# Key products of cross-attention's memory around the mixer's output projection, and decode rows broadcast by TensorE, in a one-layer decoder step

## The chip, the cores and the metric

The kernel runs on one core of one Trainium2 chip, in one launch. The metric is the device time of that launch in microseconds (us). The program has five instruction streams: PE (TensorE, matrix products; its weight loads are shown apart as PEld), DVE (VectorE, elementwise work and reductions), ACT (ScalarE, copies, casts, activations), POOL (GpSimd) and SP (SyncE, which here only issues DMA transfers). Each works through its own instructions in program order and waits on semaphores where it needs what another has made. Matrix products land in PSUM, which has eight banks of 128 partitions by 512 float32; all else is in SBUF or in DRAM.

## The reference

One step of a one-layer hybrid decoder trunk in float32, for a prompt of 512 tokens and 8 decode rows (one token each), 2048 features. Prompt and decode rows pass the weights together, as 520 columns.

```python
y, new = mixer(rmsnorm(x, w['g_mix']), ...)          # w_in, RG-LRU and mLSTM groups, w_out
x = x + y
x = x + cross_attn(rmsnorm(x, w['g_xattn']), mk, mv, w)
hf = rmsnorm(x, w['g_ffn'])
x = x + jnp.square(jax.nn.relu(hf @ w['w_up'])) @ w['w_down']

def mem_kv(mem, w):                                  # prompt only: 256 memory tokens
    mn = rmsnorm(mem, w['g_mem'])
    return (mn @ w['w_mk']).reshape(B, 256, 4, 512), (mn @ w['w_mv']).reshape(B, 256, 4, 512)

def cross_attn(h, mk, mv, w):                        # 4 heads of 512
    q = (h @ w['w_cq']).reshape(B, T, 4, 512)
    s = einsum('bthd,bnhd->bhtn', q, mk) * 512 ** -0.5
    p = softmax(s, axis=-1)
    return einsum('bhtn,bnhd->bthd', p, mv).reshape(B, T, 2048) @ w['w_co']
```

The prompt attends to keys and values made in this step from `mem_prompt` (`w_mk`, `w_mv`, also returned). The 8 decode rows attend to given caches `K` and `V` of 256 tokens each, one cache for each row.

## The kernel before, in words

**Precision.** Each float32 operand is split into a high part (rounded to fp32r) and a low part (the rest); a product is three matmuls: high by high, high by low, low by high. The high part is made by a copy on ACT, the low part by a subtraction on DVE. A weight tile is 128 x 1024 (512 KB); `split_weights` makes its pair (ACT L97, DVE L98).

**Stages.** `run_jobs` does `w_in` (82 jobs of 48 matmuls, L162) with the RG-LRU and mLSTM work between them as generators in `tasks`; one call of `step_tasks` before each job takes each a step further. Its SBUF tiles come from `slots`, 36 buffers of one tag; `hh` (the mLSTM output, two a head), `og`, `ta` and `tb` are among them. `pair_out` spills each finished pair of feature blocks to DRAM (`td["out"]`, L709 to L713). Then `rest` runs a list of jobs, `seq`: `w_out`, `w_cq`, keys and values of the memory, `w_co`, `w_up`, and four groups of `w_down`.

The big projections use Strassen's scheme with seven products for each two-by-two block (`strassen`): a unit is seven jobs, a job is 24 matmuls of 128 x 260 (`product`, L900). Each product needs its operand set (`set_load`): two batches of four feature-block pairs, each read from DRAM (520 KB, L824), copied (ACT L825) and subtracted (DVE L818) into tiles of the pool `ops` (28 buffers, `op_tile`). All seven sets of a stage, 28 tiles, stay for the whole stage. `w_out` has eight units, so have `w_cq` and `w_co`. In a stage's last unit, `leave` loads the next stage's set into the tiles that a product has just used; `set_tail` fills in the last unit's own part. The results accumulate in three PSUM tags, `acca`, `accb`, `accc`, two banks each; `ax` has two more. A unit's first product is evacuated (into `x` by DVE L907, or by ACT L918) before its third may add to the same bank.

**Order of transfers.** Every load and store is issued by SP, in one order. Weight tiles (`raw`, L844, seven buffers) are fetched one unit ahead, two jobs ahead they are split (`LOOK`). The order of all instructions on each engine is fixed when the program is built, by priorities: what stands in `high_priority` goes forward.

**Keys and values.** For each head in turn: eight jobs for the keys (`mk_job`, L1087: 24 matmuls of 256 columns, four blocks of 128 features, result `mkx[h]` kept in SBUF and stored to the output), then eight for the values (`mv_job`, L1110: 12 matmuls of 512 columns). The memory's own operands `mact` (8 tiles) are loaded in `w_cq`'s last unit (`mem_load`).

**Attention.** When a head's keys are done, `attn_prompt(h)` starts as a task: it loads the queries back (L1129), makes scores (L181), softmax, transposed probabilities, and, when the head's values and the decode are done, the weighted values; `mixed` and `spill` write `w_co`'s operands. For the decode rows, `attn_decode` takes one row of one cache at each step: `fetch` loads a cache tile (512 KB, `kv`, three buffers, L1026) and the row's query or probabilities, read from DRAM once for every partition (`qb`, two buffers, L1025); DVE multiplies and sums (L1035 for K, two of 512; L1054 for V, four of 256). `DRATE` is its steps for a job of cost 1: a product has cost 0.2, a key or value job 1.0. It begins when `w_cq`'s second unit is done. After the last value job `att_left` runs what is left of the tasks and then loads all of `w_co`'s sets.

## Time and profile before

| | us |
|---|---|
| median of 3 runs | 2968.2 (2967.15 to 2971.34) |
| the profiled execution | 2964.66 |
| its span, first to last instruction | 2962.9 |
| PE busy | 2700.3 (91% of the span) |
| PEld busy | 2626.2 (89%) |
| DVE busy | 2294.6 (77%) |
| ACT busy | 1344.3 (45%) |
| DMA, q1: 528.51 MB | 54.0% of 16 engines |

The profile shows one execution. Busy times of an engine are sums over its instructions; PE's are partly modelled, since matmuls overlap, and a matmul that starts late or at a lower granted clock counts as longer. A row of a group reads: line, engine, operation, tile written and tiles read, shape, count; then busy time, mean ns of one, and the idle time of the engine just before them with what ended it. A row of waits reads: who waited for whom, us in all, times, the longest. A row of windows has, for one stretch, the busy time of each engine with its instruction count, PE's granted clock, the share of the 16 DMA engines, and GB/s. In a timeline or a chain each row begins with start and length in us.

### The profile page before, as it was taken

To read this page: it belongs to the slowest core of one execution; us is meant where nothing else is said; L and a number is where in the kernel's file an instruction comes from. 1 tells how busy PE (TensorE), PEld (TensorE's weight loads), DVE (VectorE), ACT (ScalarE), POOL (GpSimd) and SP (SyncE) were. 2 spreads that over 40 slices of the span, in tenths; PEclk is the share of its full clock that TensorE was granted. 3 is DMA by queue.
4 is the path that set the end of the run, shared out by engine and by line. 5 is a ranking of instruction groups with operands and counts; after the bars stand their busy time and mean duration, and the time that the engine had idled before them with its cause. 6 is when DMAs were issued, how large, how long until landed. Compare 5 with 4: busy or idle time off the path is not lost.

```text
span 2962.9 us, 51442 instructions
## 1 busy us (share of the span) xinstructions
PE 2700.3 (91%) x20990; PEld 2626.2 (89%) x20990; DVE 2294.6 (77%) x3458; ACT 1344.3 (45%) x1759; POOL 31.3 (1%) x32
## 2 busy tenths in 40 slices
PE   7999999969979976796998999999998999989996
PEld 7999999968979955585997999999998989989896
DVE  7777887748878766666789777777778888887886
ACT  3444556425454421244445554554554343443543
POOL 2000000000000000000000000000000000000001
PEclk8999999989989988897998999999999999999998
DMA  4566542456666688884566655455457353443532
GB/s 142 184 212 206 187 152 87 152 200 200 197 215 213 196 260 262 276 279 164 189 208 241 203 165 164 147 162 165 148 166 261 100 201 100 151 143 107 187 108 79
DMA packets 224645, 531.80 MB, mean 179 GB/s; under 512 B 23692, under 2 KB 97132, under 8 KB 224408
## 3 DMA queue, kind: packets, MB, share of 16 engines
q1 hardware_dynamic: 224408, 528.51, 54.0%
q8 instruction: 165, 2.70, 0.4%
q14 instruction: 72, 0.59, 0.1%
HBM read 421.83 MB, written 106.73 MB: 178 GB/s over the span
## 4 chain that ended last, share of the span: by engine, by line
PE 66%; DVE 13%; DMA 12%; issue 4%; ACT 4%; SPq 1%; DVEq 0%; ACTq 0%; POOL 0%; POOLq 0%
PE acca L900 30%; PE accc L900 15%; PE mm L162 9%; PE accb L900 8%; DVE wlo L98 3%; DVE op L818 2%; DMA qb<-dp 1%; ACT whi L97 1%; DMA op<-tdd 1%; PE mv L1110 1%; DMA raw<-in_w_mv 1%; PE ax L181 1%; DVE raws L798 1%; DMA kv<-in_V 1%; PE mk L1087 1%
## 5 line engine op out<-in xcount | busy, mean ns | idle before, releaser
L900 PE MATMUL acca<-op,whi 128*128 128x260 f32 x5632 | 1051.3, 286 | 82.5 <-ACT t L918 20.2
L900 PEld LDWEIGHTS acca<-op,whi 128*128 128x128 f32 x5632 | 881.8, 190 | 92.0 <-DVE op L818 24.2
L900 PE MATMUL acca<-op,wlo 128*128 128x260 f32 x2816 | 804.1, 286 | 4.1 <-DVE wlo L98 3.9
L97 ACT CAST whi<-raw 128x1024 fp32r<-128x1024 f32 x416 | 436.4, 1050 | 607.0 <-PE acca L900 183.1
L98 DVE TENSOR_TENSOR wlo<-raw,whi 128x1024 fp32r<-128x1024 f32 x416 | 508.2, 1222 | 111.5 <-ACT whi L97 107.9
L900 PEld LDWEIGHTS acca<-op,wlo 128*128 128x128 f32 x2816 | 537.4, 191 | 5.0 <-DVE wlo L98 4.9
L900 PE MATMUL accc<-op,whi 128*128 128x260 f32 x2816 | 524.2, 284 | 11.3 <-DVE op L818 7.6
L97 ACT CAST whi<-raws 128x1024 fp32r<-128x1024 f32 x264 | 276.9, 1049 | 425.0 <-PE accc L900 137.7
L162 PE MATMUL mm<-xa,whi 128*128 128x260 f32 x2624 | 439.8, 289 | 21.3 <-ACT ssq L321 7.3
L900 PEld LDWEIGHTS accc<-op,whi 128*128 128x128 f32 x2816 | 439.5, 190 | 14.6 <-DVE op L818 9.8
L98 DVE TENSOR_TENSOR wlo<-raws,whi 128x1024 fp32r<-128x1024 f32 x264 | 322.9, 1223 | 134.2 <-ACT whi L97 133.8
L900 PE MATMUL accc<-op,wlo 128*128 128x260 f32 x1408 | 399.6, 284 | 0.7 <-DVE wlo L98 0.7
L162 PEld LDWEIGHTS mm<-xa,whi 128*128 128x128 f32 x2624 | 370.6, 192 | 26.1 <-DVE xa L310 7.4
L900 PE MATMUL accb<-op,whi 128*128 128x260 f32 x1408 | 272.3, 292 | 28.3 <-DVE op L818 16.7
L162 PE MATMUL mm<-xa,wlo 128*128 128x260 f32 x1312 | 270.8, 288 | 1.6 <-DVE wlo L98 1.6
L900 PEld LDWEIGHTS accc<-op,wlo 128*128 128x128 f32 x1408 | 266.8, 189 | 1.0 <-DVE wlo L98 0.9
L900 PEld LDWEIGHTS accb<-op,whi 128*128 128x128 f32 x1408 | 226.2, 195 | 32.5 <-DVE op L818 19.6
L162 PEld LDWEIGHTS mm<-xa,wlo 128*128 128x128 f32 x1312 | 206.3, 192 | 2.4 <-DVE wlo L98 2.1
L900 PE MATMUL accb<-op,wlo 128*128 128x260 f32 x704 | 203.4, 289 | 0.0
L818 DVE TENSOR_TENSOR op<-op,op 128x1040 fp32r<-128x1040 f32 (+2 forms) x132 | 156.6, 1190 | 26.6 <-ACT op L825 18.1
L97 ACT CAST whi<-wraw 128x1024 fp32r<-128x1024 f32 x82 | 85.5, 1045 | 151.0 <-PE mm L162 122.2
L825 ACT CAST op<-op 128x1040 fp32r<-128x1040 f32 x112 | 113.7, 1018 | 86.8 <-DMA op<-tdd 43.5
(328 smaller groups left out, 3097.7 us busy)
## 6 DMA issues: line engine op xcount, KB each, us to landing
raw<-in_w_up SPq DMA_DIRECT2D x128, 512.0 KB
raw<-in_w_down SPq DMA_DIRECT2D x128, 512.0 KB
wraw<-in_w_in SPq DMA_DIRECT2D x80, 512.0 KB
tdd<-w SPq DMA_DIRECT2D x32, 1040.0 KB
op<-tdd SPq DMA_DIRECT2D x56, 520.0 KB
raw<-in_w_out SPq DMA_DIRECT2D x32, 512.0 KB
raw<-in_w_cq SPq DMA_DIRECT2D x32, 512.0 KB
kv<-in_K SPq DMA_DIRECT2D x32, 512.0 KB
```

The costliest lines, as they stand in the source:

```text
L97: S.copy(hi, raw)
L98: V.tensor_tensor(out=lo, in0=raw, in1=hi.bitcast(F32), op=ALU.subtract)
L162: PE.matmul(ps[:, hf, 0:HT], w[:, j, :], x[:, HALF[hf]], start=(k == 0 and wi == 0), stop=(k == n - 1 and wi == 2))
L181: PE.matmul(out, u, v, start=first and i == 0, stop=last and i == 2)
L798: V.tensor_tensor(out=out, in0=x, in1=y, op=op)
L818: V.tensor_tensor(out=lo, in0=src, in1=hi.bitcast(F32), op=ALU.subtract)
L825: S.copy(hi[:, 0:n], lo[:, 0:n].bitcast(F32))
L900: PE.matmul(out, u[:, k], x[:, j], start=(new and k == 0 and i == 0), stop=(k == 7 and i == 2), skip_group_check=not new)
L1087: PE.matmul(st["mk"], u[:, i, :], x, start=(k == 0 and wi == 0), stop=(k == KB - 1 and wi == 2))
L1110: PE.matmul(st["mv"][i], x[:, ms], u[:, j], start=(k == 0 and wi == 0), stop=(k == KB - 1 and wi == 2))
```

## The change

Four things go together.

- The products for keys are taken out of the heads' order. Eight of the sixteen blocks (`MKEYS`) run before `w_out`, eight between `w_out` and `w_cq`. Each result goes through one buffer `sq` to the output and to DRAM (`dmk`). The memory's operands are loaded three times instead of once: before each key block and again in `w_cq`'s last unit. Of `w_out`'s and `w_cq`'s seven sets, five are loaded before or during a key block and two after it (`late_sets`), since the memory's tiles take eight of the 28 buffers.
- Decode rows are no longer read from DRAM for every partition. Queries and probabilities are split once a head (`rows_split`), and for each row TensorE writes it to all 128 partitions of an `acca` bank by two matmuls with one column of an identity, broadcast (`spread`); DVE reads it from PSUM. `qb` is gone, `kv` has four buffers, `t` two. `DRATE` is 1.5, and a value job has cost 1.5.
- Scores are a task of their own (`attn_scores`), two heads ahead of the weighted values at most (`attn_values`); both begin with the first value job. `w_co`'s first half of the sets is loaded before the last head's weighted values, the second after them, and two tails are filled from SBUF.
- In `w_in`, `slots` has 28 buffers; `hh` has a pool of eight of its own, `og`, `ta` and `tb` come from `kv`'s six.

```diff
-SLOTS = 36
+SLOTS = 28
...
-DRATE = 2.0
+DRATE = 1.5
+MKEYS = 8
...
+    phh = part1.enter_context(tc.tile_pool(name="phh", bufs=8))
...
-        hh = [slot("hh") for _ in range(2)]
+        hh = [phh.tile([P, T], F32, tag="hh", name=nm("hh")) for _ in range(2)]
...
-        ta, tb = slot("ta"), slot("tb")
+        ta, tb = stream((P, T)), stream((P, T))
...
-            t = slot("og")
+            t = stream((P, T))
...
+        def batch_load(key, s, b, n=4):
+            hi, lo = op_tile(), op_tile()
+            load(lo[:, 0:n].bitcast(F32), td[key][b][:, s, 0:n])
+            S.copy(hi[:, 0:n], lo[:, 0:n].bitcast(F32))
+            lo_of(lo[:, 0:n], lo[:, 0:n].bitcast(F32), hi[:, 0:n])
+            sets.setdefault((key, s), []).append((hi, lo))
...
+                if nxt == "cq":
+                    st["wcq"] = st_["w"]
+                    set_tail(nxt, 3, st_["w"], slots=SLOT_OF[:5])
+                else:
+                    set_tail(nxt, 3, st_["w"])
...
+            def leave(s):
+                p = SLOT_OF.index(s)
+                if nxt != "cq":
+                    set_load(nxt, s, 3)
+                elif p < 2:
+                    mem_load(2 * p)
+                    mem_load(2 * p + 1)
+                else:
+                    set_load(nxt, SLOT_OF[p - 2], 3)
+
...
-            enter("b", t=3, kv=3, qb=2, r=1, sm=1)()
+            enter("b", t=2, kv=4, r=1, sm=1)()
...
-            def fetch(b, rows, n, src):
-                q, t = tl("qb", (P, 512)), tl("kv", (P, 1024))
-                load(q[:, 0:n], rows_of(rows, b * n, n))
-                load(t, src[h, b].rearrange("p a b -> p (a b)"))
-                return q, t
-
-            cur = [fetch(b, dqd[h], 512, a["K"]) for b in range(2)]
+            sc = sm_tile("sc", (P, 2, NB))
+
+            def rows_split(n, src, dst):
+                hi, lo = (sm_tile("row" + c, (NB, 512), F32R)[:, 0:n] for c in "hl")
+                if dst is None:
+                    load(lo.bitcast(F32), src)
+                    src = lo.bitcast(F32)
+                S.copy(hi, src)
+                lo_of(lo, src, hi)
+                return hi, lo
+
+            def fetch(b, src):
+                t = tl("kv", (P, 4 * HT))[:, 0:1024]
+                load(t, flat(src[h, b]))
+                return t
+
+            def spread(rows, b, n):
+                ps = pacc.tile([P, 512], F32, tag="acca", name=nm("row"))[:, 0:n]
+                for i, r in enumerate(rows):
+                    PE.matmul(ps, identr[0:NB, b:b + 1].to_broadcast([NB, P]), r, start=i == 0, stop=i == 1)
+                return ps
+
+            q = rows_split(512, dqd[h], None)
+            cur = [fetch(b, a["K"]) for b in range(2)]
             for b in range(NB):
                 yield
-                qb, kt = cur.pop(0)
+                kt, qb = cur.pop(0), spread(q, b, 512)
                 for i in range(2):
                     t = kt[:, i * 512:(i + 1) * 512]
                     V.tensor_tensor_reduce(out=t, in0=t, in1=qb, op0=ALU.mult, op1=ALU.add,
                                            scale=1.0, scalar=0.0, accum_out=sc[:, i, b:b + 1])
                 if b + 2 < NB:
-                    cur.append(fetch(b + 2, dqd[h], 512, a["K"]))
-            for _ in range(4):
+                    cur.append(fetch(b + 2, a["K"]))
+            cur = [fetch(b, a["V"]) for b in range(2)]
+            for _ in range(2):
                 yield
             tp = ax()
             for i in range(2):
                 PE.transpose(out=tp[0:NB, i * P:(i + 1) * P], in_=sc[:, i], identity=ident)
-            pd = stage["sm"].tile([NB, NMEM], F32, tag="pd", name=nm("pd"))
+            pd = sm_tile("pd", (NB, NMEM))
             softmax(tp[0:NB, 0:NMEM], NB, pd)
-            dp = dram.tile([NB, NMEM], F32, name=nm("dp"))
-            load(dp, pd)
-            cur = [fetch(b, dp, NMEM, a["V"]) for b in range(2)]
+            p = rows_split(NMEM, pd, True)
+            yield
             for b in range(NB):
                 yield
-                pb, vt = cur.pop(0)
+                vt, pb = cur.pop(0), spread(p, b, NMEM)
                 for j in range(4):
                     t = vt[:, j * NMEM:(j + 1) * NMEM]
-                    V.tensor_tensor_reduce(out=t, in0=t, in1=pb[:, 0:NMEM], op0=ALU.mult, op1=ALU.add,
...
+        dmk = [dram.tile([P, 4, NMEM], F32, name=f"dmk{h}") for h in range(4)]
...
-        def mk_post(h, j, g):
+        def mk_post(n, g):
             if g:
-                if j == 0:
-                    mkx[h] = op_tile((P, 4, NMEM), F32)
-                t = mkx[h][:, j]
+                t = tl("sq", (P, NMEM))
                 V.tensor_tensor(out=t, in0=st["mk"], in1=rm, op=ALU.mult)
-                load(o["mk"][4 * h + j], t)
-                if j == 3:
-                    start(attn_prompt(h))
+                load(o["mk"][n], t)
+                load(dmk[n // 4][:, n % 4], t)
 
...
         def mv_post(h, g):
             if g == 7:
-                mvx[h] = op_tile((P, 2, 512), F32)
+                while h > 1 and not pv_done[h - 2]:
+                    step_tasks()
+                t = tl("kv", (P, 4 * HT))[:, 0:1024].rearrange("p (a b) -> p a b", a=2)
                 for i in range(2):
-                    t = mvx[h][:, i]
-                    S.activation(t, st["mv"][i], AF.Copy, scale=rmc[:, i:i + 1])
-                    load(o["mv"][h, i], t)
+                    S.activation(t[:, i], st["mv"][i], AF.Copy, scale=rmc[:, i:i + 1])
+                    load(o["mv"][h, i], t[:, i])
+                mvx[h] = hi, lo = op_tile((P, 2, 512)), op_tile((P, 2, 512))
...
+        def attn_scores():
+            for h in range(4):
+                while h > 1 and not pv_done[h - 2]:
+                    yield
...
+                pTs[h] = pT
+
+        def attn_values():
+            for h in range(4):
+                while not (adec_done[h] and h in mvx and h in pTs):
+                    yield
...
+                        wa, wb = (op_tile(dt=F32) if h < 3 else tl("kv", (P, 4, HT)) for _ in range(2))
...
+                pv_done[h] = True
+
+        def att_enter():
+            start(attn_scores())
+            start(attn_values())
 
         def att_left():
+            while not (pv_done[2] and 3 in pTs):
+                step_tasks()
+            for s in SLOT_OF:
+                batch_load("co", s, 0)
             while tasks:
                 step_tasks()
-            for _, _, s in ORDER:
-                set_load("co", s, 3)
-            set_tail("co", 3, *wlast)
+            for s in SLOT_OF:
+                batch_load("co", s, 1, 2)
+            for j in range(2):
+                set_tail("co", 2 + j, *wlast[j])
...
+        def keys(n0, n1):
+            plain([a["w_mk"][n, g] for n in range(n0, n1) for g in range(2)],
+                  lambda g, w: mk_job(n0 + g // 2, g % 2, w), lambda g: mk_post(n0 + g // 2, g % 2))
+
+        def late_sets(key, last):
+            def go():
+                for s in SLOT_OF[5:]:
+                    set_load(key, s, last)
+                if last < 4:
+                    set_tail(key, 3, st["wcq"], slots=SLOT_OF[5:])
+            return go
+
+        def mem_again(s):
+            p = SLOT_OF.index(s)
+            if p < 2:
+                mem_load(2 * p)
+                mem_load(2 * p + 1)
+
+        keys(0, MKEYS)
+        seq[-1]["after"] = late_sets("out", 4)
+        strassen("out", 8, sq_src("w_out"), **residual(0, 1, C_X, "cq"))
+        keys(MKEYS, KB)
+        seq[-1]["after"] = late_sets("cq", 3)
+        strassen("cq", 8, sq_src("w_cq"), ev_q, cq_enter, mem_again)
+        first = len(seq)
         for h in range(4):
-            plain([a["w_mk"][4 * h + j, g] for j in range(4) for g in range(2)],
-                  lambda g, w, h=h: mk_job(h, g // 2, g % 2, w), lambda g, h=h: mk_post(h, g // 2, g % 2))
             plain([a["w_mv"][h, g] for g in range(8)],
                   lambda g, w, h=h: mv_job(h, g, w), lambda g, h=h: mv_post(h, g))
+        seq[first]["enter"] = att_enter
...
+        enter("a", x=2, w=2, sq=1, ss=1)()
         for q in range(4):
             fetch(0, q)
-        for _, _, s in ORDER:
-            set_load("out", s)
+        for k4 in range(4):
+            mem_load(k4)
         for n in range(LOOK):
             prep(n)
+        for s in SLOT_OF[:5]:
+            set_load("out", s)
```

More of the change, by code (lines that the diff above doesn't have):

```diff
@@ L72, in stream @@
     def stream(shape):
-        return small.tile(list(shape), F32, tag="kv", name=nm("kv"), bufs=6)
+        return small.tile([P, T], F32, tag="kv", name=nm("kv"), bufs=6)[:, 0:shape[1]]
     def aux():
@@ L270, in tile_trunk @@
     rm = keep.tile([P, NMEM], F32, name="rm")
+    identr = keep.tile([NB, NB], F32R, name="identr")
     drows = dram.tile([4, 3, TP], F32, name="drows")
@@ L818, in lo_of, with set_tail @@
             V.tensor_tensor(out=lo, in0=src, in1=hi.bitcast(F32), op=ALU.subtract)
-        def set_load(key, s, last=4):
-            out = []
-            for b, n in ((0, 4), (1, last)):
-                hi, lo = op_tile(), op_tile()
-                load(lo[:, 0:n].bitcast(F32), td[key][b][:, s, 0:n])
-                S.copy(hi[:, 0:n], lo[:, 0:n].bitcast(F32))
-                lo_of(lo[:, 0:n], lo[:, 0:n].bitcast(F32), hi[:, 0:n])
-                out.append((hi, lo))
-            sets[key, s] = out
-        def set_tail(key, j, wa, wb=None):
-            for _, _, s in ORDER:
+        def batch_load(key, s, b, n=4):
[4 more added lines that the diff above has]
+            sets.setdefault((key, s), []).append((hi, lo))
+        def set_load(key, s, last=4):
+            batch_load(key, s, 0)
+            batch_load(key, s, 1, last)
+        SLOT_OF = [s for _, _, s in ORDER]
+        def set_tail(key, j, wa, wb=None, slots=SLOT_OF):
+            for s in slots:
                 src = wa[:, s] if wb is None or s < 4 else wb[:, s - 4]
@@ L996, in q_decode @@
                 PE.transpose(out=tp[0:NB, i * P:(i + 1) * P], in_=t[:, 1 + i, HT - NB:HT], identity=ident)
-            qd = stage["sm"].tile([NB, 256], F32, tag="qd", name=nm("qd"))
+            qd = sm_tile("pd", (NB, 256))
             S.copy(qd, tp[0:NB, 0:256])
@@ L1002, in q_decode, with sm_tile @@
                 start(attn_decode_all(), DRATE)
+        def sm_tile(tag, shape, dt=F32, bufs=1):
+            return stage["sm"].tile(list(shape), dt, tag=tag, name=nm(tag), bufs=bufs)
         def softmax(ps, rows, out):
-            mx, su = (stage["sm"].tile([P, 1], F32, tag=n, name=nm(n), bufs=4)[0:rows] for n in ("mx", "su"))
+            mx, su = (sm_tile(n, (P, 1), bufs=4)[0:rows] for n in ("mx", "su"))
             V.reduce_max(out=mx, in_=ps, axis=AX.X)
@@ new lines, in attn_values @@
+        def attn_values():
+            for h in range(4):
+                while not (adec_done[h] and h in mvx and h in pTs):
+                    yield
+                mv, pT = mvx[h], pTs[h]
+                odh = sm_tile("odh", (P, 4, NB))
+                V.tensor_tensor(out=odh, in0=od[:, 4 * h:4 * h + 4], op=ALU.mult,
+                                in1=scl[:, None, DEC].to_broadcast([P, 4, NB]))
+                for j in range(4):
+                    ps = ax()
+                    for i in range(2):
+                        three(ps, part(mv, slice(None), i, slice(j * P, (j + 1) * P)), part(pT, slice(None), i),
+                              i == 0, i == 1)
+                    if j % 2 == 0:
+                        wa, wb = (op_tile(dt=F32) if h < 3 else tl("kv", (P, 4, HT)) for _ in range(2))
+                    for c in range(2):
+                        n = (HT, TP - HT)[c]
+                        o_ = wa[:, 3 - c if j % 2 else c]
+                        V.tensor_tensor(out=o_[:, 0:n], in0=ps[:, c * HT:c * HT + n],
+                                        in1=scl[:, c * HT:c * HT + n], op=ALU.mult)
+                        if c:
+                            S.copy(o_[:, n:HT], odh[:, j])
+                    if j % 2:
+                        mixed(wb, wa)
+                        k = 2 * h + j // 2
+                        if h < 3:
+                            spill("co", k, wa, wb)
+                        else:
+                            wlast.append((wa, wb))
+                        yield
+                pv_done[h] = True
@@ L1273, in sq_src @@
             return lambda u, i, j: a[name][2 * u + i, 0, j]
-        strassen("out", 8, sq_src("w_out"), enter_=enter("a", x=2, w=2, sq=1, ss=1),
-                 **residual(0, 1, C_X, "cq"))
-        strassen("cq", 8, sq_src("w_cq"), ev_q, cq_enter, mem_load)
         def plain(srcs, run, post):
```

128 lines of the change are left out of this document (49 added, 79 removed).

## The prediction

> **What bounds the kernel now.** I read the page's busy slices first, then the windows cut at the stage boundaries, then in each stage the chain and the waits.
>
> ```profile
> PE   7999999969979976796998999999998999989996
> DMA  4566542456666688884566655455457353443532
> ```
>
> Slices 14 to 18, the attention block, are where PE falls to 6 and 7 tenths while DMA stands at 8. The windows say how much that is. I cut them at the last product of each stage: `w_out` 629 to 832, `w_cq` to 1023, keys, values and attention to 1366, `w_co` to 1566.
>
> ```profile
> core 0: us, PE busy (x) PEld busy (x) DVE busy (x) ACT busy (x) POOL busy (x), PEclk, DMA share, GB/s
> 629.00:832.00 203.00, 173.75 (x1342) 170.25 (x1343) 163.47 (x196) 94.69 (x105) 0.00 (x0) 0.91 0.65 221
> 832.00:1023.00 191.00, 171.47 (x1369) 169.27 (x1368) 156.74 (x205) 91.44 (x126) 0.00 (x0) 0.94 0.56 192
> 1023.00:1366.00 343.00, 269.03 (x1487) 225.93 (x1485) 228.02 (x600) 107.89 (x164) 0.00 (x0) 0.89 0.78 257
> 1366.00:1566.00 200.00, 171.55 (x1340) 169.44 (x1341) 155.64 (x196) 90.11 (x106) 0.00 (x0) 0.90 0.61 204
> 700.00:830.00 130.00, 129.69 (x1071) 129.52 (x1071) 114.75 (x142) 63.30 (x72) 0.00 (x0) 1.00 0.68 223
> ```
>
> A busy PE hides waiting here, so I price the work by undisturbed runs of the chain (start, length, what):
>
> ```profile
> 768.04 5.81 PE acca L900 x48
> 1289.65 3.47 PE mv L1110 x15
> 1305.56 5.34 PE ax L181 x23
> 1310.90 14.74 PE mk L1087 x125
> ```
>
> One Strassen product of 24 matmuls is 2.91 us, so a stage of 56 needs 163 us. `w_out` takes 203, `w_cq` 191, `w_co` 200: 40, 28 and 37 us are lost, nearly all near their starts (the row 700:830 has PE busy throughout). A matmul costs 0.118 us with 256 columns and 0.232 with 512. Keys are 768 of the first (90.6 us), values 384 of the second (88.8), scores 192 of the first (22.6), attention's values 96 of the second (22.3): 224 us of work in a stage of 343. So 119 us are lost there, and 224 in the four stages. After 1566 the change touches nothing, before 629 only the tile buffers.
>
> Why they are lost, by the waits (us, times, longest) of the attention block, then of `w_cq`'s start and `w_co`'s start:
>
> ```profile
> ACT whi L97 <- DMA raw<-in_w_mv: 56.6, 15, 7.7
> ACT whi L97 <- DMA raw<-in_w_mk: 47.8, 12, 19.7
> ```
> ```profile
> PE acca L900 <- ACT t L918: 13.7, 1, 13.7
> ```
> ```profile
> PE acca L900 <- DVE x L907: 14.1, 1, 14.1
> ```
>
> ScalarE waits 104 us for weight tiles to land. They are late because one queue issues every load in order, and its own waits name the decode rows:
>
> ```profile
> SPq L1025 <- DVE od L1054: 35.8, 19, 3.0
> SPq L844 <- DVE wlo L98: 30.1, 16, 4.0
> SPq L1025 <- DVE sc L1035: 27.5, 12, 2.8
> ```
>
> L1025 loads a broadcast row into one of two `qb` buffers; until VectorE has read the old one, the weights behind it are not issued either. `w_out` starts late for another reason, in PE's and then SP's order of time:
>
> ```profile
> 628.54 0.40 PE L162 MATMUL mm<-xa,wlo 128*128 128x260 f32 x2
> 644.79 0.58 PE L900 MATMUL acca<-op,whi 128*128 128x260 f32 x1 [15.85 <-ACT op L825]
> ```
> ```profile
> 633.05 0.40 SPq L713 DMA_DIRECT2D tdout<-tb  x1
> 633.54 2.80 SPq L844 DMA_DIRECT2D raw<-in_w_out  x4
> ```
>
> The operand sets need the last pair's spill, and PE has nothing else to do.
>
> **The change part by part.** The rows of the attention block that carry VectorE's load:
>
> ```profile
> L98 DVE TENSOR_TENSOR wlo<-raw,whi 128x1024 fp32r<-128x1024 f32 x64 | 78.3, 1223 | 32.7 <-ACT whi L97 32.3
> L1054 DVE CUSTOM_DVE_ANT_0 kv<-kv,qb 128x256 f32<-128x256 f32 x126 | 46.3, 421 | 28.4 <-DMA qb<-dp 14.5 <-DMA kv<-in_V 11.9 <-DVE op L1095 0.7
> L1035 DVE CUSTOM_DVE_ANT_0 kv<-kv,qb 128x512 f32<-128x512 f32 x48 | 31.3, 689 | 26.6 <-DMA kv<-in_K 17.9 <-DMA qb<-dqd 8.7
> L1095 DVE TENSOR_TENSOR op<-mk,rm 128x256 f32<-128x256 f32 x16 | 6.7, 421 | 2.1 <-PE mk L1087 1.9
> ```
>
> *Keys ahead of `w_out` and of `w_cq`.* Each block is 8 x 48 matmuls at 0.118 = 45.3 us of PE. It leaves the attention block and covers the set loads. It is not free of loss: in block 1 there must land 16 weight tiles of 512 KB (8.4 MB), five sets of two 520 KB loads (5.3), the next four weight tiles (2.1), and 16 stores of 128 KB go out (2.1): 17.9 MB. The rate sustained in a full stretch is
>
> ```profile
> 1200.00:1290.00 90.00, 69.54 (x385) 59.75 (x384) 61.45 (x160) 29.06 (x43) 0.00 (x0) 0.87 0.87 302
> ```
>
> 302 GB/s, so 59 us against 45: 14 us lost. The ends are 4 (the first weights and the memory's tiles land before 629, since `hh`, `og`, `ta`, `tb` leave the slots) and 26 (they come after the last spill as at 633.54, 12 us more). So 629 to `w_out`'s end is 45.3 + 163 + 14 = 222 against 203: +19. VectorE's load there, 30 subtractions of 1.22 us, is 37 of 45 us and hidden; without that cover it is on the path. In block 2 the loads begin a unit earlier (`leave`), 65 us for some 19 MB, so bandwidth costs nothing; `r1` and the tail are ready before `w_cq` begins, which removes the 13.7 us wait, but sets six and seven are loaded only after the block, in front of products at +14.5 and +17.4 us. I take 10, ends 5 and the old 28. With 8 rows spread in `w_cq` (4 us): 45.3 + 163 + 4 + 10 = 222 against 191: +31.
>
> The single `sq` buffer makes each key's evacuation wait for the two stores of the one before; there are 5.7 us between them. The queue carries those 16 stores twice (once more for `dmk`), eight loads of the memory's tiles more and four of keys, and 54 `qb` loads and four `dp` stores less. I cost the buffer at nothing; a store held on the queue would stop VectorE and so `wlo`.
>
> *Decode rows through TensorE, and scores ahead of values.* The block's transfers:
>
> ```profile
> DMA packets 36464, 88.07 MB, mean 257 GB/s; under 512 B 3529, under 2 KB 16086, under 8 KB 36441
> ...
> raw<-in_w_mk SPq DMA_DIRECT2D x24, 512.0 KB
> ...
> qb<-dqd SPq DMA_DIRECT2D x24, 256.0 KB
> ...
> qb<-dp SPq DMA_DIRECT2D x30, 128.0 KB
> ```
>
> Decode progress before is 0.4 steps a product, afterwards 0.3, about 11 in `w_cq`: again the first head's 8 rows of K, so 48 and about 128 reductions stay in this block. At 2.25 steps a job the other 70 steps take 31 of the 32 value jobs, so decode ends with them. VectorE: 228.0 less 32 `wlo` of the keys (39.1) and their evacuation (6.7), plus eight row splits (0.4 to 0.7 each, 4): 187 us. PE: 224 - 90.6 + 24 rows x 2 x 0.232 + 32 x 2 x 0.118 = 152. DMA: 88.1 - 12.6 (keys' weights) - 10.2 (24 x 256 KB and 30 x 128 KB) - 2.1 (key stores) + 2.1 (keys read back) = 65 MB, 215 us at 302 GB/s. So VectorE and DMA bound the block, not PE. VectorE's best long stretch with PE undisturbed is 114.75 of 130 us, 0.883: 187 / 0.883 = 211 us, beside DMA's 215. If nothing loosens, the block keeps its 228 / 343 = 0.665: 281 us. With no `qb` behind which weights queue, and four `kv` buffers for two fetches ahead, I take `w_cq`'s 156.74 / 191 = 0.82, the nearest stage with decode in it: 228 us against 343, -115.
>
> What the spread adds: PE now waits, in order, for VectorE's release of an `acca` buffer, and the value matmuls stand behind it. It is inside the 211 to 281. In `w_cq` the other `acca` buffer serves as well; a row that waits for its K tile there holds the next unit's first product (inside the 5 to 28).
>
> The reductions now read PSUM. The rows of the same addition from PSUM and from SBUF:
>
> ```profile
> L907 DVE TENSOR_TENSOR x<-acca,x 128x260 f32<-128x260 f32 x192 | 81.3, 424 | 42.6 <-PE acca L900 41.3 <-DMA x<-dx 0.6
> L798 DVE TENSOR_TENSOR t<-t,t 128x260 f32<-128x260 f32 x16 | 6.8, 423 | 0.2
> ```
>
> 424 and 423 ns: I add nothing. [...]
>
> *`w_co`'s start.* The 14.1 us wait is for the residual `x`, loaded at
>
> ```profile
> 1406.15 0.80 SPq L928 DMA_DIRECT2D x<-dx  x2
> ```
>
> behind fourteen set loads, in space that the last `t` tiles held. Those now lie in `kv`, half of the set loads goes out before the last values, and behind them come the other half and two tails for each set. I take 16 lost instead of 37 (ends 8 and 37): 179 against 200, -21.
>
> *Fewer slots before 629.* 28 instead of 36, with `hh` in its own pool.
>
> ```profile
> 45.00:345.00 300.00, 290.41 (x2314) 285.99 (x2314) 224.42 (x555) 146.30 (x277) 3.09 (x10) 0.97 0.58 187
> 345.00:445.00 100.00, 96.73 (x771) 94.65 (x769) 85.96 (x193) 57.89 (x97) 0.00 (x0) 1.00 0.48 150
> ```
>
> In the second row all eight `hh` already sit in the 36, leaving 28, and PE idles 3.3 in 100 us; in the first, with up to 34, 9.6 in 300. I take +4, between 0 and a doubling of these 13.
>
> Sum: 19 + 31 - 115 - 21 + 4 = -82. The profiled execution took 2964.7 us (span 2962.9), 3.5 under the median of 2968.2; 2964.7 - 82 + 3.5 = 2886. All good ends: 212 + 217 + 211 + 171 = 811 against 937, -126, 2842. All bad ones: 234 + 240 + 281 + 200 + 13 = 968, +31, 2999.
>
> **The rivals.** (1) *The attention block keeps its pace.* Each of 56 rows couples PE and VectorE both ways where a `qb` load coupled SP and VectorE; the block stays at 0.665, 281 us. Then -82 + 53 = -29: 2939. For it: VectorE idled 28.4 + 26.6 us at the reductions, 30 us of that for `kv` tiles that are still loaded. Against: the 63 us that the queue waited at L1025 go with `qb`. (2) *Slower: the row spread becomes the wait.* Place: the `acca` pair, in PE's in-order queue. Price: 82 us over 56 rows; from 1.5 us a row beyond the forecast (the block at 310 us, VectorE at 0.60) the gain is gone, and at 2 us a row it gives 2998. Against: it needs a lower VectorE share than today with less to transfer. (3) *The cover does not cover:* weights and memory tiles come behind the last spill, block 1 and block 2 lose 26 and 28: 2886 + 12 + 18 = 2916.
>
> **How the numbers follow.** Forecast 0.5 (2845 to 2905 by its own), rival 3 alone 0.16 (2916), rival 1 0.2 (2939), rival 2 0.08 (about 2998), and 0.06 for rivals 1 and 3 together, 2969, which is no change within 0.2%, about what this kernel's measurement can tell. So faster 0.86, same 0.06, slower 0.08. Predicted 2886; 2845 to 2945 leaves out some 0.19.
>
> **What would show it.** Right: `mk` matmuls directly behind 629 with PE idle under 5 us, PE busy throughout both key blocks, no `qb` transfers, VectorE above 0.8 and weight waits under 40 us in a value block of about 228 us, `w_co` under 180. Wrong: PE waiting for reductions before the spread matmuls (rivals 1 and 2), `raw<-in_w_mk` issued after the last spill (rival 3), or PE idle before 445 well above 13 us.

## The result, and the profile after

The changed kernel's median is 2870.29 us (four executions: 2860.84, 2861.05, 2879.53 and 2880.28) against 2967.68 us for the kernel before on the same chip, a ratio of 0.967 [0.963, 0.972]: some 97 us faster, where the prediction had 82 and 2886 us. Two later series of runs gave 0.971 [0.970, 0.973] and 0.971 [0.968, 0.974]. The profiled execution took 2861.05 us, with a span of 2859.1.

The busy slices of the changed kernel's page first, then its windows, cut at the same events as before (columns: span and length of the stretch, busy time of PE, PEld, DVE, ACT and POOL with instruction counts, granted clock, DMA share, GB/s).

```profile
PE   7999999989999999978979999999998999999996
DMA  3566642377768458885667555454556353433532
```
```profile
626.00:852.00 226.00, 211.18 (x1728) 209.24 (x1727) 184.38 (x219) 111.89 (x122) 0.00 (x0) 0.97 0.72 237
852.00:1078.00 226.00, 221.40 (x1773) 214.90 (x1773) 186.20 (x230) 113.30 (x146) 0.00 (x0) 0.99 0.63 214
1078.00:1291.00 213.00, 189.28 (x825) 137.27 (x824) 182.37 (x564) 78.32 (x140) 0.00 (x0) 0.93 0.85 293
1291.00:1468.00 177.00, 167.23 (x1363) 166.26 (x1362) 158.29 (x209) 93.02 (x118) 0.00 (x0) 0.97 0.63 207
```

The dip of the attention block is gone; what is left of it is the slice from 1215 to 1287 us, the 18th digit, at 7 tenths, which holds most of the tail spoken of below. The four stages were 203, 191, 343 and 200 us and are now 226, 226, 213 and 175 (the last window ends 2 us behind `w_co`'s last product). The first two took the keys in and grew by 23 and 35 us, less than the 45.3 us of each key block's matmuls; the attention block lost 130 us where the keys account for 91 of it.

The same cut was made in every kernel below, exactly at the events: the last `w_in` matmul; the 1344th and the 2688th Strassen matmul (56 products of 24 in each stage); `w_co`'s first; `w_co`'s last. "Tail" is the part of the attention block behind the last value matmul. All are us, from one profiled execution each.

| kernel | `w_in` ends | `w_out` + block 1 | `w_cq` + block 2 | attention block | of it tail | `w_co` | rest | span |
|---|---|---|---|---|---|---|---|---|
| before | 628.9 | 203.5 | 191.2 | 342.0 | 9.7 | 200.9 | 1396.3 | 2962.9 |
| after | 626.1 | 226.3 | 225.3 | 213.3 | 27.7 | 175.1 | 1393.0 | 2859.1 |
| after_again | 625.4 | 228.5 | 223.6 | 215.5 | 27.5 | 175.0 | 1404.8 | 2872.8 |
| after_beside_e8 | 626.4 | 230.5 | 223.9 | 213.3 | 28.0 | 174.5 | 1404.5 | 2873.1 |
| e1 rows by DMA | 629.0 | 228.6 | 219.1 | 261.4 | 43.2 | 177.9 | 1398.5 | 2914.4 |
| e7 keys in block | 626.8 | 197.3 | 190.5 | 334.9 | 9.6 | 173.3 | 1398.0 | 2920.9 |
| e2 scores not ahead | 627.3 | 227.0 | 224.8 | 211.6 | 33.1 | 180.8 | 1403.5 | 2875.0 |
| e3 all keys before `w_out` | 626.1 | 273.3 | 189.9 | 219.0 | 28.0 | 173.5 | 1395.1 | 2876.9 |
| e4 decode at 2.0 | 628.1 | 227.8 | 225.0 | 211.0 | 9.5 | 174.1 | 1399.6 | 2865.5 |
| e5 36 slots | 626.0 | 233.0 | 222.2 | 221.0 | 27.5 | 174.0 | 1401.8 | 2877.9 |
| e6 own space | 628.8 | 213.4 | 227.1 | 219.3 | 26.5 | 179.0 | 1388.4 | 2856.0 |
| e8 e4 and e6 | 624.8 | 216.1 | 228.0 | 215.0 | 8.1 | 176.9 | 1389.0 | 2849.8 |
| e9 `w_co` sets late | 626.2 | 227.4 | 226.6 | 214.5 | 27.8 | 174.3 | 1397.3 | 2866.4 |
| e10 one pass | 624.4 | 227.5 | 222.3 | 212.1 | 26.6 | 174.4 | 1397.1 | 2857.8 |

Between the two profiled executions: -2.8, +22.8, +34.1, -128.7, -25.8, -3.3, together -103.7 us. The three executions of the changed kernel show how far to trust a row: the four stages sum to 840.0, 842.6 and 842.2, while the rest, in which the code is the same, ranges from 1393.0 to 1404.8, with a granted clock of 0.98 in the first and 0.97 in the other two. So a difference of a few us is read from the stages, and a whole time differing by 10 us may be nothing.

In the attention block, the waits of the changed kernel (who waits for whom: us, times, longest), then SP's own:

```profile
ACT whi L99 <- PE mv L1139: 42.8, 17, 5.1
```
```profile
SPq L1060 <- DVE od L1095: 33.6, 16, 5.0
SPq L1060 <- DVE sc L1076: 23.6, 10, 4.4
```

ScalarE no longer waits 104 us for weight tiles; it waits for PE. SP still waits 57 us for VectorE, as it did at the `qb` loads, but now at L1060, the cache tile's own load, two rows ahead of need and with four buffers: the queue is held, and yet no cast of ScalarE in this block waits for a weight tile.

The groups that changed (line, engine, operation, tiles, shape, count, then busy time, mean ns of one, and the idle time before them):

```profile
L1095 DVE CUSTOM_DVE_ANT_0 kv<-kv,row 128x256 f32<-128x256 f32 x128 | 46.5, 412 | 3.3 <-PE row L1066 3.3
L1076 DVE CUSTOM_DVE_ANT_0 kv<-kv,row 128x512 f32<-128x512 f32 x48 | 31.8, 681 | 2.5 <-PE row L1066 2.5
L1066 PE MATMUL row<-rowh,identr 8*128 8x256 f32 (+1 forms) x56 | 24.8, 455 | 14.9 <-ACT rowh L1054 8.0 <-DVE od L1095 6.4 <-DVE sc L1076 0.5
L1066 PE MATMUL row<-rowl,identr 8*128 8x256 f32 (+1 forms) x56 | 19.3, 363 | 0.5 <-DVE rowl L823 0.5
```

VectorE idles 5.8 us ahead of its reductions instead of 55.0. The price is 44.1 us of PE in 112 small matmuls, where the prediction had reckoned 18.7 from column counts.

### The profile page after: what moved, and what is told of

Same layout as the page of the kernel before. It is cut to its first block, busy times and chain, and to the rows that moved or that the text cites. A ratio compares the mean times of both kernels' runs of the same rounds, so it can differ in the third digit from the quotient of the medians.

```text
span 2859.1 us, 51798 instructions
## 1 busy us (share of the span) xinstructions
PE 2697.8 (94%) x21118; PEld 2612.8 (91%) x21118; DVE 2301.2 (80%) x3481; ACT 1357.9 (47%) x1783; POOL 31.3 (1%) x32
## 4 chain that ended last, share of the span: by engine, by line
PE 76%; DVE 10%; DMA 8%; issue 3%; ACT 3%; SPq 1%; DVEq 0%; ACTq 0%
PE acca L908 32%; PE accc L908 16%; PE mm L164 11%; PE accb L908 8%; DVE wlo L100 3%; PE mv L1139 3%; PE mk L1119 2%; DVE op L823 2%; PE ax L183 1%; DMA op<-tdd 1%; PE row L1066 1%; ACT whi L99 1%; PE aux L183 1%; DMA op<-dmem 1%; DMA out_s_C<-ct 1%
## 5 line engine op out<-in xcount | busy, mean ns | idle before, releaser
L164 PE MATMUL mm<-xa,whi 128*128 128x260 f32 x2624 | 439.4, 289 | 22.8 <-DVE xa L312 10.8
L908 PE MATMUL accb<-op,whi 128*128 128x260 f32 x1408 | 263.9, 286 | 17.6 <-DVE op L823 10.1
L823 DVE TENSOR_TENSOR op<-op,op 128x1040 fp32r<-128x1040 f32 (+3 forms) x136 | 159.5, 1177 | 29.1 <-ACT op L1106 15.1
L828 ACT CAST op<-op 128x1040 fp32r<-128x1040 f32 (+1 forms) x112 | 112.5, 1005 | 86.6 <-DMA op<-tdd 47.5
```

Of the source, the lines that this page charges most:

```text
L164: PE.matmul(ps[:, hf, 0:HT], w[:, j, :], x[:, HALF[hf]], start=(k == 0 and wi == 0), stop=(k == n - 1 and wi == 2))
L823: V.tensor_tensor(out=lo, in0=src, in1=hi.bitcast(F32), op=ALU.subtract)
L828: S.copy(hi[:, 0:n], lo[:, 0:n].bitcast(F32))
L908: PE.matmul(out, u[:, k], x[:, j], start=(new and k == 0 and i == 0), stop=(k == 7 and i == 2), skip_group_check=not new)
```

## The experiments

Theories to be told apart: where the attention block's gain comes from (rows, keys, scores ahead), what bounds the block now, what the key blocks cover, and where their own losses come from. Times are compared with the kernel before in the same series of runs (a job, in the expectations): 2962.58 us (e1, e2, e3, after_again), 2964.97 (e4 to e7), 2961.63 (e8 to e10, after_beside_e8).

**The changed kernel, twice more.**

> The changed kernel once more, beside the kernels of the same job, since its runs fell in two groups (2860.84 and 2861.05, 2879.53 and 2880.28 us). Every theory: 2855 to 2882 us, 0.963 to 0.972 of the kernel before, and stages of 226, 226, 213 and 177 us from the end of w_in within 3 us each.

> The changed kernel, to compare the others of this job with. Every theory: 0.965 to 0.973 of the kernel before, block 213 to 216 us, w_co 175 us.

Measured 2877.38 and 2873.8 us, and the stages as in the table, within 5 us of the first in each.

**e1: rows by DMA again.**

```diff
-            enter("b", t=2, kv=4, r=1, sm=1)()
+            enter("b", t=2, kv=4, qb=2, r=1, sm=1)()
...
-                kt, qb = cur.pop(0), spread(q, b, 512)
+                qb, kt = cur.pop(0)
...
-                    cur.append(fetch(b + 2, a["K"]))
+                    cur.append((row(dqd[h], b + 2, 512), fetch(b + 2, a["K"])))
```

> The decode rows come by broadcast DMA into a tile of two buffers again instead of being spread by TensorE; all else is the changed kernel. Theory A (the rows' DMAs were what held the weights and VectorE in the old attention block, so that the spread is what lets the block run at 0.94 of TensorE): the block goes from 213 to 240 to 265 us, waits of the whi casts for weight tiles come back with over 40 us, VectorE falls below 0.75 in it, and the kernel takes 2890 to 2915 us. Theory B (the block gained because the key products left it and the scores run ahead; how the rows come is indifferent, since the spread takes some 29 us of TensorE, 56 rows at 0.45 to 0.65 us, that the DMA would give back): the block stays within 205 to 222 us and the kernel within 8 us of the changed one.

2910.34 us, 0.982 [0.980, 0.985]; the block takes 261.4 us. Its window, and two of its waits:

```profile
1077.00:1338.00 261.00, 163.73 (x700) 124.42 (x698) 181.11 (x552) 73.71 (x129) 0.00 (x0) 0.82 0.82 270
```
```profile
ACT whi L99 <- DMA raw<-in_w_mv: 37.5, 12, 11.8
DVE kv L1085 <- DMA qb<-dp: 32.7, 18, 6.1
```

Theory A, though the weight waits, 37.5 us, stay a little under its 40: the same VectorE work (181 against 182 us) takes 46 to 48 us longer, the weight waits are back, and VectorE waits for its rows. The 44 us that the spread costs PE are well spent. The edit also fetches a head's first two V tiles after the softmax instead of before it, as their rows must be in DRAM first; the tail, 43.2 us against 27.5 to 28.0, holds 15 of the 46 to 48 us.

**e7: keys in the attention block again, rows by TensorE.**

```diff
-        keys(0, MKEYS)
-        seq[-1]["after"] = late_sets("out", 4)
...
-        keys(MKEYS, KB)
-        seq[-1]["after"] = late_sets("cq", 3)
...
         for h in range(4):
+            keys(4 * h, 4 * h + 4)
             plain([a["w_mv"][h, g] for g in range(8)],
...
-                while h > 1 and not pv_done[h - 2]:
+                while mk_done[h] < 4 or h > 1 and not pv_done[h - 2]:
```

> The key products stand in the attention block again, four blocks each ahead of its head's values, with the rows spread by TensorE as in the changed kernel and no block before w_out or w_cq. With the kernel before (keys in the block, rows by DMA), the kernel with rows by DMA (keys outside) and the changed kernel this closes a square. w_out and w_cq take about 395 us together in every theory, as in the kernel before. Theory A (the rows were the attention block's only trouble; the keys' place gives just the cover of two stage starts): the block takes the 215 us of the changed one and some 97 us for the 768 key matmuls, 305 to 318 us, w_co 175 to 180, the kernel 2900 to 2920 us. Theory B (keys among the values hold the block up by themselves, since each head's scores then wait for its keys): the block takes 325 to 345 us, against 342 in the kernel before, and the kernel 2925 to 2950 us.

2919.0 us, 0.984 [0.981, 0.987]; the block takes 334.9 us, only 7 under the kernel before.

```profile
1014.00:1349.00 335.00, 300.98 (x1598) 244.01 (x1597) 233.57 (x614) 112.60 (x173) 0.00 (x0) 0.89 0.73 250
```
```profile
ACT whi L99 <- PE mk L1121: 103.4, 27, 10.5
ACT whi L99 <- PE mv L1142: 42.3, 19, 9.0
```

The block's length is theory B's, the kernel's time theory A's, since `w_co` is 28 us shorter here too (below). The rows' waits are gone and so are the weights'; ScalarE waits for PE throughout, and neither VectorE (0.70) nor DMA (0.73) is full. So with the spread alone the block no longer waits for weights, and yet saves next to nothing: PE is counted busy for 301 of 335 us. That is 31 us more than the changed kernel's 213 and 91 for the keys' matmuls. The granted clock, 0.89 here against 0.93 there, may account for much of it: by (1 - clock) times length some 37 against 15 us of PE's time (an estimate from the two windows). Why the clock was lower, and where the other 9 us are, isn't settled.

Put together, the two projections and the attention block take 736.7 us in the kernel before, 722.7 with the spread and the keys in place (-14), 709.1 with the keys moved and rows by DMA (-28), and 664.9 to 667.7 with both (-69 to -72). (The three changed ones share the rest of the change, so "before" is not quite a corner of the square.) The two parts are worth more together than apart by 27 to 30 us. That each removes the limit that the other one runs into fits the waits (for weights and rows in e1, for PE in e7); as the granted clock was lower in both (0.82 and 0.89 against 0.93), part of the surplus may be the clock's.

**e2: scores no longer ahead.**

```diff
-                while h > 1 and not pv_done[h - 2]:
+                while h > 0 and not pv_done[h - 1]:
```

> The scores of head h wait for the values of head h-1 again instead of h-2; all else is the changed kernel. Theory A (the attention block is bound by what TensorE and VectorE have to do, 0.94 and 0.85 of the stretch of the value matmuls): the scores still have room, the block stays within 4 us of 213 and the kernel within 5 us. Theory B (running ahead is what keeps the softmax of the next head off the path): TensorE stands at each of three head changes for a softmax of 4 to 10 us, the block takes 12 to 30 us more.

2878.44 us against 2877.38; the block 211.6 us against 215.5:

```profile
1079.00:1291.00 212.00, 187.54 (x802) 135.03 (x799) 179.11 (x552) 76.09 (x133) 0.00 (x0) 0.90 0.86 304
```

Theory A. The same load of VectorE and DMA in the same time: that the scores run two heads ahead is worth nothing that can be measured here.

**e3: all keys before `w_out`.**

```diff
-MKEYS = 8
+MKEYS = 16
```

and no second block, with `w_cq` entered as in the kernel before.

> All 16 key products stand ahead of w_out in one block, none between w_out and w_cq, whose start is as in the kernel before. Theory A (a block of products ahead of a weight stage covers that stage's first weights, and w_cq lost 28 us at its start without one): the first two stages together take 452 + 20 to 28 = 472 to 480 us instead of 452, the kernel 2880 to 2890 us. Theory B (the products' place is indifferent, the gain came from their leaving the attention block, where they stood behind VectorE's work): the two stages together stay within 6 us of 452. In both the block ahead of w_out starts with the same wait of some 12 us for the memory's tiles.

2882.89 us against 2877.38, ratios 0.974 [0.972, 0.975] and 0.971 [0.970, 0.973]. The first two stages together take 463.2 us against 452.1: 11 us, between both theories. The whole times are too close to tell apart. The cover of the second block is real, but worth half of what I expected: without it `w_cq` takes 189.9 us, 27 more than its 163 of products, as in the kernel before (28), but with it the two still lose 223.6 - 45.3 - 163 = 15. The eight key blocks that were moved cost 273.3 - 228.5 = 44.8 us ahead of `w_out`, just their matmuls. `w_cq`'s start without a block ahead of it, from PE's waits in this kernel:

```profile
PE acca L908 <- ACT t L926: 6.6, 1, 6.6
```

That was 13.7 us in the kernel before. This wait is 7 us shorter by something else in the change, but the stage hardly is (189.9 against 191.2); it now holds the spread of the first head's rows as well, which may take up the difference.

**e10: one pass of the spread left out.**

```diff
-                for i, r in enumerate(rows):
-                    PE.matmul(ps, identr[0:NB, b:b + 1].to_broadcast([NB, P]), r, start=i == 0, stop=i == 1)
+                for i, r in enumerate(rows[:1]):
+                    PE.matmul(ps, identr[0:NB, b:b + 1].to_broadcast([NB, P]), r, start=True, stop=True)
```

> The spread leaves out the rows' low part: 64 of its 128 matmuls, so the decode rows are rounded; all else is the changed kernel. The low part takes 19.3 us of TensorE in the attention block. Theory A (TensorE, 0.94 busy in the stretch of the value matmuls, bounds the block): the block is 12 to 20 us shorter, the kernel 12 to 20 us faster. Theory B (VectorE and DMA bound it, as the prediction had it): TensorE stands idle for the 19 us instead, the block stays within 5 us of 215 and the kernel within 5 us.

2861.06 us against 2873.8, with intervals that overlap ([0.964, 0.970] and [0.968, 0.974]). Taken alone the time speaks for theory A; the stages do not. The block:

```profile
1074.00:1287.00 213.00, 183.80 (x778) 134.21 (x778) 180.85 (x566) 79.89 (x143) 0.00 (x0) 0.90 0.85 294
```

It is 212.1 us against 213.3 to 215.5, the stretch of the value matmuls 185.4 against 185.3 to 188.1: theory B. The two profiled executions of this series are 15.3 us apart, and 7.4 of them are in the rest, which the edit doesn't touch. But the test is weaker than it was meant to be: matmuls that counted as 19.3 us busy left, and PE's busy time fell by 5.5 only, with a granted clock of 0.90 in the block against 0.93 ((0.93 - 0.90) x 213 = 6 us of PE's time, an estimate). VectorE and DMA hold 0.85 each. Which of the three engines binds wasn't separated.

**e4: the decode rows faster.**

```diff
-DRATE = 1.5
+DRATE = 2.0
```

> The decode task is stepped at 2.0 instead of 1.5 rows a job; all else is the changed kernel, whose attention block has a tail of 27.5 us behind the last value matmul, in which the last head's rows are done. Theory A (the rows were only paced too slowly): the tail falls to 8 to 15 us, the block goes from 215 to 198 to 206 us, the kernel is 8 to 18 us faster. Theory B (TensorE at 0.94 and VectorE at 0.85 bound the stretch of the value matmuls, so rows pulled forward lengthen it by as much): the tail falls, the stretch of the value matmuls grows from 188 to 195 us or more, the block stays within 4 us of 215 and the kernel within 5 us.

The last head's rows lie behind the last value matmul in the changed kernel, at the end of a chain through the softmax; its window there (1263 to 1291) and PE's wait:

```profile
1263.00:1291.00 28.00, 14.59 (x45) 10.02 (x44) 25.11 (x88) 7.58 (x14) 0.00 (x0) 0.63 0.92 312
```
```profile
1270.97 0.79 PE L1066 MATMUL row<-rowh,identr 8*128 8x256 f32 x2 [6.75 <-ACT rowh L1054]
```

In e4 the stretch of the value matmuls and the tail are:

```profile
1081.00:1282.00 201.00, 188.59 (x796) 135.79 (x794) 170.51 (x539) 71.72 (x128) 0.00 (x0) 0.91 0.85 293
1282.00:1292.00 10.00, 8.02 (x27) 5.70 (x25) 8.02 (x11) 5.71 (x11) 0.00 (x0) 0.83 0.85 323
```

The tail falls by 18 us and the stretch ahead of it grows by 13 to 16: theory B for the block, 211.0 against 213.3 to 215.5. The tail looked like idle time of PE; VectorE was busy for 25.1 of its 28 us, and that work has to be done somewhere. The kernel's 2870.39 us, 0.968 [0.966, 0.970], was not measured beside the changed one; by the ratios (0.967 and 0.971) it lies between there and some 10 us below, which decides nothing.

**e5: the first stage's slots as before.**

```diff
-SLOTS = 28
+SLOTS = 36
...
-        hh = [phh.tile([P, T], F32, tag="hh", name=nm("hh")) for _ in range(2)]
+        hh = [slot("hh") for _ in range(2)]
```

and likewise for `ta`, `tb` and `og`.

> The part of the change in the first stage is undone: 36 slots, with hh, ta, tb and og in slots; all else is the changed kernel. Theory A (the freed space only lets the weight and row tiles be allotted, and costs or gives nothing in the first stage): w_in ends at 623 to 631 us, the kernel within 5 us of the changed one. Theory B (fewer slots make the first stage wait less or more): w_in ends 3 us or more to either side of 625 to 629, and what depends on early weight tiles shows at the key block's start, 11.8 us now, 15 to 25 us then.

`w_in` ends at 626.0 us, as it does with 28 slots: fewer slots cost nothing. But the key block starts 19.5 us after it, not 11.9, and its weights are among the waits:

```profile
PE mk L1118 <- ACT op L1105: 19.5, 1, 19.5
ACT whi L98 <- DMA raw<-in_w_mk: 8.6, 3, 7.5
```

So that part of the change buys early weight tiles, worth about 8 us at this place and 2.5 to 7 in the stage (233.0 against 226.3 to 230.5): theory A for `w_in`, theory B for the key block's start. The kernel's 2879.56 us, 0.971 [0.968, 0.974], is no different from the changed one's.

**e6: a space of its own for the memory's tiles.**

```diff
-        pops = pool("ops", 28)
+        plate = pool("late", 8)
+        pops = pool("ops", 20)
...
-            hi, lo = op_tile(), op_tile()
+            hi, lo = (op_tile(late=s in SLOT_OF[5:]) for _ in range(2))
...
-            hi, lo = op_tile((P, 4, NMEM)), op_tile((P, 4, NMEM))
+            hi, lo = (op_tile((P, 4, NMEM), late=True) for _ in range(2))
```

> The memory's tiles and the late sets come from a space of their own, 8 tiles laid ahead of the other 20, so that the memory's loads need not wait for the space of w_in's tiles; all else is the changed kernel, where the first key matmul stands 11.8 us after w_in's last. Theory A (the loads wait for space that only w_in's last matmuls free): the idle time at the key block's start falls from 11.8 to under 5 us, the kernel is 5 to 10 us faster. Theory B (they wait for something else, their turn behind the spills on the issuing queue or the cast on ScalarE): the idle time stays 9 to 13 us and the kernel within 4 us.

In the changed kernel PE's wait at the first key block, and SP's order around it:

```profile
PE mk L1119 <- ACT op L1106: 11.9, 1, 11.9
```
```profile
618.06 4.80 SPq L852 DMA_DIRECT2D raw<-in_w_mk  x4
...
630.44 0.41 SPq L718 DMA_DIRECT2D tdout<-kv  x1
630.94 0.45 SPq L852 DMA_DIRECT2D raw<-in_w_mk  x1
631.44 1.89 SPq L1105 DMA_DIRECT2D op<-dmem  x4
```

The weights are issued 8 us ahead of `w_in`'s end, the memory's tiles after it, behind the last spill. In e6:

```profile
597.42 2.03 SPq L1106 DMA_DIRECT2D op<-dmem  x3
...
612.56 0.43 SPq L1106 DMA_DIRECT2D op<-dmem  x1
...
633.54 0.54 SPq L718 DMA_DIRECT2D tdout<-kv  x1
```

Theory A: with space that does not overlap `w_in`'s tiles the loads begin 31 us ahead of `w_in`'s end instead of 5 behind it, and the first key matmul follows `w_in` by 0.9 us. The stage, between 226 and 231 us before this edit, falls to 213.4 us, which is 45.3 + 163 and 5 us. The kernel takes 2855.92 us, 0.963 [0.962, 0.965]; by the ratios that is 12 to 24 us below the changed one, more than theory A's 5 to 10.

**e8: e4 and e6 together.**

> The two edits that helped by themselves, the memory's tiles and late sets in a space of their own and the decode rows at 2.0 a job. Theory A (they act in different stages and add): the key block starts within 3 us of w_in's end, the tail is 9 to 12 us, the kernel 13 to 25 us below the changed one of this job, 0.958 to 0.964 of the kernel before. Theory B (the decode's gain is given back in the stretch of the value matmuls and only the first edit is worth anything): 9 to 13 us below it, the block at 215 to 220 us.

2852.32 us against 2873.8 in the same series, 0.963 [0.961, 0.966] and 0.971 [0.968, 0.974]. It is the fastest kernel here, and 21.5 us are within theory A's 13 to 25. But e6 alone has the same ratio, and the block takes 215.0 us: theory B for the decode rate. The gain is larger than theory B's 9 to 13 us all the same. From the table, 10.3 us come from the first two stages and 15.5 from the rest, which is 1389.0 us here and 1388.4 in e6, against 1393.0 and more everywhere else. The granted clock doesn't explain the shorter rest: it was 0.97 there in e6 and e8, as in after_again. Dividing the space also changes which tiles the later stages take; whether that is what shortened the rest stays open.

**e9: half of `w_co`'s sets later.**

```diff
-            for s in SLOT_OF:
-                batch_load("co", s, 0)
             while tasks:
                 step_tasks()
+            for s in SLOT_OF:
+                batch_load("co", s, 0)
```

> The first half of w_co's sets is loaded after the attention's tasks are done, as both halves were in the kernel before, not ahead of them; all else is the changed kernel. Every changed kernel so far ran w_co in 173 to 181 us, whatever was undone, against 200.9 before. Theory A (that gain comes from loading half of the sets before the tail): the tail and w_co together go from 202.5 to 215 to 228 us, the kernel 12 to 25 us slower. Theory B (the gain comes from the last pairs that are kept on chip, and from less waiting of VectorE there): tail and w_co stay within 5 us of 202.5.

2868.47 us, 0.969 [0.966, 0.972]; tail and `w_co` 202.1 us, unchanged. It fits theory B, but decides less than it should, for the order on SP is the same with and without the edit. In the changed kernel, then in e9:

```profile
1281.88 9.67 SPq L827 DMA_DIRECT2D op<-tdco  x11
```
```profile
1285.59 8.56 SPq L827 DMA_DIRECT2D op<-tdco  x11
```

Both runs of loads go out 9.1 to 9.2 us ahead of `w_co`'s first product (1291.0 and 1294.8). Something else holds them until then, so loading half of the sets ahead of the tail buys no time in this kernel.

## Why the prediction was right, and where it was not

*The attention block* (forecast 228 us, measured 213). The part on the rows held: in e1 weights and VectorE wait for them again, and the block is 46 to 48 us longer. VectorE's work was 182.4 us (187 forecast, where the forecast's own terms add up to 186), the block's transfers 293 GB/s x 213 us = 62.4 MB (65), VectorE's share 0.86 where I had taken 0.82. That VectorE and DMA bound the block, and not PE, is not shown: they are busy for 0.86 and 0.85, PE is counted busy for 0.89, and e10 took too little off PE to decide. e4 shows only that the decode work costs as much ahead of the last value matmul as behind it. The block's length also went with the granted clock. after_again and e5 run the same code in it:

```profile
1077.00:1293.00 216.00, 193.24 (x831) 139.61 (x830) 182.69 (x564) 78.72 (x142) 0.00 (x0) 0.91 0.84 290
1081.00:1302.00 221.00, 197.54 (x828) 143.01 (x826) 183.23 (x565) 79.25 (x141) 0.00 (x0) 0.88 0.82 283
```

With 0.93, 0.91 and 0.88 of the clock and the same VectorE work the block takes 213.3, 215.5 and 221.0 us. The prediction has no term for the clock: by (1 - clock) times length, an estimate from the windows, PE lost 38 us to it in the block before and 15 after, 23 of the 129 us by which the block is shorter. Which is cause and which effect was not tested. The forecast is for both parts of the change together and doesn't say that neither does it alone, as e1 and e7 show. Rival 1, the old pace of 0.665, is close to what e1 shows with rows by DMA: 181.11 / 261 = 0.69.

*The spread's price on PE.* 18.7 us by column counts, 44.1 in the profile; by e10 half of it is worth 1 to 3 us of the block. The mis-sized term did not spoil the sum, as the block still came out 15 us under the forecast; that it lies beside VectorE's work, as I had put it, fits e10 without being settled by it. Rival 2 (the `acca` pair becomes the wait) shows as 6.9 us of PE waiting for reductions, against a price of 82 us.

*Reductions from PSUM.* They take 412 and 681 ns, against 421 and 689 from SBUF before. I had added nothing, and nothing was needed: each is 8 or 9 ns shorter than before.

*Block 1* (forecast +19, measured +22.8). The sum nearly held by luck: I wrote 14 us for bandwidth, and e6 runs the same transfers with 5 us lost. The real loss is 11.9 us for the memory's tiles, which I had named only as the bad end and as half of rival 3. That rival came half true, with the weights early and the memory's tiles late; "PE idle under 5 us" was wrong. The step that failed is "the first weights and the memory's tiles land before 629, since `hh`, `og`, `ta`, `tb` leave the slots": e5 shows that this frees the weights' space, e6 that the memory's tiles lie in space freed later.

*Block 2* (forecast +31, measured +34.1). PE is busy in 221.4 of 226 us, and the 13.7 us wait is gone. Yet e3 shows that only 11 us hang on the block's place, as `w_cq` loses 27 us without a block ahead of it and the two still lose 15 with it.

*`w_co`* (forecast 179, measured 175.1). PE's wait for the residual `x` falls from 14.1 to 2.0 us, its waits for the operand sets from 14.4 to 7.7, and the granted clock in the stage was 0.97 against 0.90. The two loads of `x` are now issued 30 and 21 us ahead of `w_co`'s first product, not 40 behind it:

```profile
1261.10 0.71 SPq L936 DMA_DIRECT2D x<-dx  x1
...
1269.91 0.43 SPq L936 DMA_DIRECT2D x<-dx  x1
```

Every variant of the changed kernel ran `w_co` in 173 to 181 us, whichever of rows, keys, scores or slots was undone. So the gain belongs to none of these. That most of it comes from `x` having space early fits the order on SP and the missing wait, but no run isolated it.

*Decode ends with the value jobs.* Wrong: the last head's eight rows of V lie behind the last value matmul, a tail of 28 us. I counted steps, not the chain from the last K row through softmax and split to the first V row, on which PE waits 6.75 us. e4 shows that it costs next to nothing, since VectorE fills the tail.

*Fewer slots* (forecast +4, measured -2.8) cost nothing, by e5. *The single `sq` buffer*, costed at nothing, held PE's key matmuls for 1.4 us in both key blocks together.

## What to carry to other kernels

When one queue issues all loads, look for a small transfer that waits for a consumer: part of what it costs may be found in the late weights behind it (37.5 us of ScalarE's waits in e1). Here the rows were some 10 of the block's 88 MB, and making them on chip took 46 us off the changed kernel's block. Moving independent work out of a stage may not pay fully while the stage's next limit stays: moving the keys gave 28 us with the rows by DMA, the spread 14 with the keys in place, and both together 69 to 72. So test both parts apart before adding up their gains. And check in which space a block's first operands lie: here the work placed to cover loads waited 11.9 us itself, and 0.9 us when its tiles no longer overlapped those of the stage before.

## What the runs showed that was not expected

The busy time of the small matmuls was not their price. In e10, leaving out matmuls with 19.3 us in the attention block took 5.5 us off PE's busy time in it and 1 to 3 us off its length. Of the 14 us between these two counts some 6 go with the lower granted clock in that execution (an estimate, worked out at e10); 8 don't.

The mean granted clock over an execution went with the kernel: 0.950 to 0.960 in the kernel before beside e8, 0.969 to 0.977 in the changed kernel, 0.957 to 0.967 in e1 and e7, which leave PE more gaps (in the windows of the four stages PE isn't busy for 127 and 78 us, against 53 in the changed kernel). It also went with the spread among executions of one kernel: of the changed kernel's first four, the two near 2861 us had 0.977 and 0.974, the two near 2880 us 0.970 and 0.969. But one execution of e5 had 0.925 and took 2879.48 us, as long as one with 0.972 (2879.64 us), so the mean alone does not give the time. That the gaps are the reason was not tested.
